# Hybrid SSD/attention/MoE block: half of adaLN's second part moves from TensorE products to VectorE products

## The chip, the cores and the metric

One core of a Trainium2 chip runs the whole block: one sequence of 256 tokens, width 1024, all arrays float32 in memory, batch 1. The metric is the device time of one execution in microseconds. Three runs of the kernel before gave 686.21, 688.96 and 686.09 us (median 686.21 us).

## The reference

```python
def _hybrid_layer(h, c, ...):
    ada = silu(c) @ w_ada + b_ada                 # c: 1 x 1024, w_ada: 1024 x 6144
    shift1, scale1, gate1, shift2, scale2, gate2 = split(ada, 6)
    hn = rmsnorm(h, norm1_g) * (1 + scale1) + shift1
    z, xbc, dt, q, kc, vc, ks, vs, kw, vw, gn, gs, ga = split(hn @ w_in)   # w_in: 1024 x 9040
    y_ssm = mamba2_mixer(z, xbc, dt, ...) @ w_ssm_out     # 4 groups of 8 heads, chunks of 128
    y_nsa = nsa_mixer(q, kc, ...) @ w_nsa_out             # 16 heads; compressed, selected, window
    merged = sigmoid(gs) * y_ssm + sigmoid(ga) * y_nsa
    h = h + gate1 * (merged @ w_o)
    hn2 = rmsnorm(h, norm2_g) * (1 + scale2) + shift2
    return h + gate2 * hier_moe(hn2, ...)                 # 32 experts of hidden 256, top 2
```

The first part of adaLN (shift1, scale1) is needed before anything else can run. The second part, the 4096 columns of gate1, shift2, scale2 and gate2, is needed only from the residual (gate1) and the router and experts (the other three) on. The change concerns these 4096 columns: one row vector of 1024 times a 1024 x 4096 matrix, 16 MB of weights.

## The kernel before, in words

**Stages.** The kernel runs in this order: adaLN's first part and the first columns of `hn @ w_in`; q, k, v (`pj` banks, L612); the last of `xbc` with rope beside it (L1105 to L1107); then one long list of items (L1168 to L1327) in which TensorE computes the projections z, gs, ga, then `no` (w_nsa_out), `so` (w_ssm_out) and `wo` (w_o); then the router; then 16 pairs of experts.

**Items.** A projection of 256 columns ("unit", 1 MB of weights) is two items, one for each 128 columns (`fm_items`, L544). An item first has its weights split (`split`, L216) into a high part on ScalarE (`wh`, L227) and the rest on VectorE (`wl`, L228, 128 x 1024); then 24 matmuls of 128 x 256 run on TensorE (L563 to L565). `project` (L524) traces the split of an item two items ahead of its matmuls. There are three buffers for `wl`.

**Side work.** Beside the items runs one chain of generators (L1105): rope, compression, dt, the compressed attention, the attention over 16 heads (`side_attn`, 36 steps and a last one), and the scan (`side_ssd`, four groups of nine steps, after each second group four more with `ssd_norm`: 44 steps). `weave` (L570) traces, behind every item, 1.5 side steps while the attention lasts (RATE_ATTN) and 1.35 after it (RATE_SSD). It counts items, whatever an item costs: an item with no projection in it, such as a unit of adaLN, also moves the side on by 1.5 or 1.35 steps. So the list of items sets how far the side work stands ahead of or behind the projections in the program.

**Order on the engines.** From this program order the framework fixes one order for each engine: of the instructions that it expects to be ready, the one traced first goes first. Up to the experts no order is written out by hand. `turn_over` (L1217), the item after the first halves of so0 to so2, traces what is left of the side work, closes the buffers of this phase and opens those for the router and experts; its first instruction on GpSimd is at L1232.

**adaLN's second part.** `ada_units` (L185) has 16 units of 256 columns: units 0 to 3 are gate1, 4 to 7 shift2, 8 to 11 scale2, 12 to 15 gate2. The units' weights are streamed two behind each z unit (L193 to L197). `ada_use` (L1142) takes one unit: `ada_rows` (L345) does eight matmuls with the column `sc` (silu(c) in one of 32 columns, the others zero) as stationary operand, on four 32-column strips of the array, into PSUM bank 7; ScalarE copies the four partial rows out (L1148), and a DMA on SP's queue writes them to `adR` in device memory (L1149). The items list has two of these behind each of z0 to z7 (L1185). Behind z7 comes `ada_out` (L1151): it loads `adR`, adds the four partial rows and the bias on 32 partitions, writes the sum to `adD` and transposes it into `a2`. `router_weights` (L1131) comes behind gs3 (L1190).

**Slots.** All weights and most large tiles share 19 slots of 1 MB (L118); a weight's DMA starts when a slot that was released earlier comes free.

Of the kernel before, what the change touches and what calls it, by code (L numbers as in the profile page):

```python
# [12 lines left out]
AF = mybir.ActivationFunctionType  # L13
OP = mybir.AluOpType
# [43 lines left out]
def tile_hybrid_block(ctx: ExitStack, tc: tile.TileContext, x, c, positions, w_ada, b_ada, norm1_g, w_in, conv_w,  # L58
# [4 lines left out]
    PE, V, A, G, SP = nc.tensor, nc.vector, nc.scalar, nc.gpsimd, nc.sync  # L63
# [10 lines left out]
    def ps(b, name):  # L74
        return psp.tile([128, 512], F32, tag=f"b{b}", name=name)

    def work(shape, tag, name, bufs=1, dt=F32):
        return wk.tile(shape, dt, tag=tag, bufs=bufs, name=name)

    def const(shape, name, dt=F32):  # L80
        return csp.tile(shape, dt, name=name)
# [4 lines left out]
    def stt(o, a, s, b, op0, op1):  # L86
        return V.scalar_tensor_tensor(o, a, s, b, op0=op0, op1=op1)  # L87

    def tt(o, a, b, op):
        return V.tensor_tensor(o, a, b, op=op)  # L90

    def ts(o, a, s1, op0, s2=None, op1=None):
        if op1 is None:
            return V.tensor_scalar(o, a, s1, None, op0=op0)  # L94
        return V.tensor_scalar(o, a, s1, s2, op0=op0, op1=op1)
# [7 lines left out]
    def mm(o, l, r, start, stop):  # L103
        return PE.matmul(o, l, r, start=start, stop=stop)  # L104
# [17 lines left out]
    def slot(name):  # L122
        tag = free.pop(0)
        tag_of[name] = tag
        return (big if tag[0] == "s" else box["xtra"]).tile([128, 2048], F32, tag=tag, name=name)

    def load_next():
        name, emit = stream[st["next"]]
        held[name] = slot(name)
        emit(held[name])  # L130
        st["next"] += 1

    def pump():
        while st["next"] < len(stream) and len(free) > st["keep"]:
            load_next()
# [5 lines left out]
    def release(*names):  # L141
        for name in names:
            free.append(tag_of.pop(name))
            held.pop(name, None)
        pump()

    def want(name):
        while name not in held:
            load_next()
        return held[name]  # L150
# [9 lines left out]
    def ld(w, width, c0, n, k0=0, nk=8):  # L160
        def f(t):
            SP.dma_start(t[:, 0:nk * n].rearrange("p (k n) -> p k n", k=nk),
                         dram(w, c0 + k0 * 128 * width, [[width, 128], [width * 128, nk], [1, n]]))
        return f
# [20 lines left out]
    ada_units = [(j, u) for j in range(2, 6) for u in range(4)]  # L185

    def ada_stream(n):
        for j, u in ada_units[n:n + 1]:
            stream.append((f"ad{j}{u}", ld(w_ada, 6144, j * 1024 + u * 256, 256)))

    zga = [(f"z{u}", O_Z + u * 256) for u in range(8)] + [(f"{nm}{u}", o + u * 256) for nm, o in
                                                          (("gs", O_GS), ("ga", O_GA)) for u in range(4)]
    for n, (nm, o) in enumerate(zga):  # L193
        stream.append((nm, ld(w_in, IN_W, o, 256)))
        if n < 8:
            ada_stream(2 * n)
            ada_stream(2 * n + 1)  # L197
    for u in range(4):
        stream.append((f"no{u}", ld(w_nsa_out, 1024, u * 256, 256)))
    for kh in range(2):  # L200
# [34 lines left out]
    def rows(q, dst, r0, src, n):  # L235
        q.dma_start(dst[r0:r0 + n, :], dram(src, 0, [[128, n], [1, 128]]))
# [11 lines left out]
    ones = const([128, 128], "ones")  # L248
# [6 lines left out]
    sc = const([128, 8, 32], "sc")  # L255
# [89 lines left out]
    def ada_rows(o, w):  # L345
        wv = w.rearrange("p (k n) -> p k n", k=8)
        for kk in range(8):
            j = kk % 4
            mm(o[32 * j:32 * j + 32], sc[:, kk, :], wv[:, kk, :], kk < 4, kk >= 4)

    def p0_rows(k, t=None):
        b = ps(6, f"ar{k}")
        if t is not None:
            behind(b, t)
        ada_rows(b[:, 0:256], want(f"ada{k}"))
        release(f"ada{k}")
        rw = work([128, 256], "w1k", f"rw{k}", 4)
        V.tensor_copy(rw, b[:, 0:256])
        return rw
# [84 lines left out]
    for k in range(8):  # L444
        if k == 3:
            T2r, T3r, dsk, posi, dtb, alb, w2k, w2v = small_loads()
        if 0 < k < 7:
            rw = p0_rows(k + 1)
        p0_mm(k, 0, *w0)
        if k == 0:  # L450
# [3 lines left out]
            rw = p0_rows(1, w0[1])  # L454
# [12 lines left out]
    b = ps(6, "cols2")  # L467
# [145 lines left out]
    items = []  # L613
# [486 lines left out]
    items = []  # L1100
    for u in range(6):
        def ev(b, u=u):
            conv_silu(*conv_taps(NP0 + 2 * u, b))
# [10 lines left out]
    def z_evac(u, b):  # L1114
        q = SZ[u // 4][:, (u % 4) * 512:(u % 4 + 1) * 512]
        A.activation(q, b, AF.Tanh, scale=0.5)
        stt(q, q, 1.0, b, OP.add, OP.mult)
# [21 lines left out]
    adR = drm.tile([4, 32, 128], F32, name="adR")  # L1139
    adD = drm.tile([32, 128], F32, name="adD")  # L1140

    def ada_use(n):  # L1142
        j, u = ada_units[n]
        b = ps(7, f"adr{n}")
        ada_rows(b[:, 0:256], want(f"ad{j}{u}"))
        release(f"ad{j}{u}")
        rw = work([128, 256], "w1k", f"rwa{n}", 4)
        A.activation(rw, b[:, 0:256], AF.Copy)  # L1148
        SP.dma_start(adR[:, 2 * n:2 * n + 2].rearrange("a r c -> a (r c)"), rw[0:128:32, :])  # L1149

    def ada_out():  # L1151
        aw = work([32, 6, 128], "wA", "aw", 4)
        V.memset(aw[:, 5], 1.0)
        SP.dma_start(aw[:, 0:4], adR.rearrange("a r c -> r a c"))
        rows(SP, aw[:, 4], 0, b_ada[0, 2048:6144], 32)
        rows(SP, aw[:, 5], 16, norm2_g, 8)
        for n in range(1, 5):
            tt(aw[:, 0], aw[:, 0], aw[:, n], OP.add)
        stt(aw[:, 0], aw[:, 0], one16, aw[:, 5], OP.add, OP.mult)
        A.dma_start(adD, aw[:, 0])  # L1160
        b = ps(7, "adT")
        PE.transpose(b[:, 0:32], aw[:, 0], ident[0:32, 0:32])
        V.tensor_copy(a2, b[:, 0:32])

    ada_items = [((lambda: None), (lambda n=n: ada_use(n)), None) for n in range(16)]

    keep(4)
    items = []  # L1168
    for n, (nm, o) in enumerate(zga):
        u = int(nm[-1])  # L1170
        if nm[0] == "z":
            items += fm_items(nm, lambda b, u=u: z_evac(u, b))
        else:
            def ev(b, u=u, nm=nm[:2]):
                if u == 0:
                    box[nm] = slot(nm + "t")
                    if not box.get("attn"):
                        keep(1 if nm == "gs" else 0)
                    elif nm == "ga":
                        keep(3)  # L1180
                A.activation(box[nm][:, u * 512:(u + 1) * 512], b, AF.Tanh, scale=0.5)
            items += fm_items(nm, ev)
            if nm == "ga3":
                items.append(((lambda: None), (lambda: release("HH", "HL")), None))
        items += ada_items[2 * n:2 * n + 2]  # L1185
        if n == 0:
            items.append(((lambda: None), router_loads, None))
        if n == 7:
            items.append(((lambda: None), ada_out, None))
        if n == 11:  # L1190
            items.append(((lambda: None), router_weights, None))

    for u in range(4):
# [200 lines left out]
    b = ps(7, "pos")  # L1394
# [518 lines left out]
```

## Time and profile before

| | before |
|---|---|
| median of 3 runs | 686.21 us |
| the profiled execution's own time | 685.09 us |
| its span, first to last instruction | 683.4 us |
| TensorE matmul busy | 640.0 us (94%) |
| TensorE weight load busy | 507.2 us (74%) |
| VectorE busy | 467.3 us (68%) |
| ScalarE busy | 327.5 us (48%) |
| mean granted TensorE clock | 0.985 |

All times below are microseconds from the first instruction of the profiled execution. Busy shares are of the span; matmuls are pipelined and their ends are modelled, so a busy TensorE can still have room, and its pace is better read from the starts of its matmuls.

### The profile page before, as it was taken

How to read it: one execution, taken by the hardware profiler on the slowest of the kernel's cores; microseconds unless marked ns; L12 is line 12 of the kernel's file. 1: busy time of each engine (PE TensorE's matmuls, PEld its weight loads, DVE VectorE, ACT ScalarE, POOL GpSimd, SP SyncE). 2: the span in 40 equal slices, each digit the busy share in tenths (PEclk: the TensorE clock that was granted, in tenths of full speed). 3: DMA queues.
4: the chain of work that ended last, by engine and by line, in shares of the span. 5: the costliest groups of instructions: out<-in, count | busy, mean ns of one | idle time of the engine just before them, and what ended most of it. 6: DMA issues, size and time to landing. Idle time of an engine off the chain costs nothing. (4 is left out here: it accounts for less than half of the span.)

```text
span 683.4 us, 14362 instructions
## 1 busy us (share of the span) xinstructions
PE 640.0 (94%) x5714; PEld 507.2 (74%) x5715; DVE 467.3 (68%) x1158; ACT 327.5 (48%) x632; POOL 7.9 (1%) x67
## 2 busy tenths in 40 slices
PE   8999999899899999999999999988988999999882
PEld 7889889897767777999899998774655655656541
DVE  3657999994788878786999766574444534555543
ACT  5435878663378667355745544452322312222333
POOL 2000000000000000000000100000000000000000
PEclk9999999999999999999999999999999999999997
DMA  8997971479667758636477998637999999999971
GB/s 267 335 336 242 370 224 54 144 236 300 208 203 252 257 173 277 195 119 237 132 253 241 345 406 299 234 106 299 419 420 420 419 420 420 418 419 419 416 315 63
DMA packets 102196, 193.28 MB, mean 283 GB/s; under 512 B 7636, under 2 KB 83940, under 8 KB 90596
## 3 DMA queue, kind: packets, MB, share of 16 engines
q1 hardware_dynamic: 101268, 191.05, 76.8%
q8 instruction: 57, 0.93, 0.6%
q10 hardware_dynamic: 848, 1.11, 0.5%
q14 instruction: 23, 0.19, 0.1%
HBM read 190.98 MB, written 1.16 MB: 281 GB/s over the span
## 5 line engine op out<-in xcount | busy, mean ns | idle before, releaser
L104 PE MATMUL moe<-g,XG 128*32 128x256 f32 (+1 forms) x560 | 69.4, 380 | 2.4 <-PEq L1590 1.1
L104 PE MATMUL moe<-u,XG 128*32 128x256 f32 (+1 forms) x560 | 69.5, 381 | 0.0
L104 PEld LDWEIGHTS moe<-g,XG 128*32 128x32 f32 (+1 forms) x560 | 39.5, 112 | 28.4 <-issue 10.0
L1575 ACT ACTIVATE moe<-moe 64x256 f32<-64x256 f32 x32 | 11.4, 356 | 67.1 <-DVE hp L94 65.3
L104 PE MATMUL moe<-d,rw 128*32 128x512 f32 (+1 forms) x280 | 38.6, 631 | 2.0 <-ACT XG L1500 1.2
L104 PE MATMUL pj_z<-HH,wl 128*128 128x256 f32 x128 | 36.5, 285 | 0.5 <-DVE wl L90 0.5
L87 DVE SCALAR_TENSOR_TENSOR hp<-hp,moe 64x256 f32<-64x256 f32 x32 | 13.4, 419 | 34.2 <-ACT hp L1611 33.8
L104 PE MATMUL pj_z<-HH,wh 128*128 128x256 f32 x128 | 36.5, 285 | 0.0
L104 PE MATMUL pj_z<-HL,wh 128*128 128x256 f32 x128 | 36.3, 283 | 0.0
L104 PEld LDWEIGHTS moe<-u,XG 128*32 128x32 f32 (+1 forms) x560 | 35.2, 112 | 0.3
L1500 ACT ACTIVATE XG<-moe,GC 128x256 f32<-128x256 f32 x36 | 18.0, 564 | 34.2 <-PE moe L104 34.2
L104 PE MATMUL moe<-DT,HFh 128*128 128x256 f32 x128 | 31.8, 298 | 2.1 <-DVE DT L90 1.1
L1611 ACT ACTIVATE hp<-moe 64x256 f32<-64x256 f32 x32 | 12.1, 379 | 43.9 <-PEq L1590 26.8
L913 ACT ACTIVATE P<-P,mn 128x128 f32<-128x128 f32 (+1 forms) x64 | 28.4, 446 | 5.2 <-DVE mn L910 4.9
L104 PE MATMUL moe<-DT,HFl 128*128 128x256 f32 x128 | 30.6, 288 | 0.2 <-DVE HFl L87 0.2
L104 PE MATMUL pj_xb<-HH,wh 128*128 128x256 f32 x96 | 27.0, 282 | 3.0 <-ACT BC L493 1.5
L104 PEld LDWEIGHTS moe<-DT,HFh 128*128 128x128 f32 x128 | 24.0, 195 | 5.6 <-issue 5.6
L104 PE MATMUL xa<-HH,wh 128*128 128x256 f32 x96 | 27.8, 293 | 0.0
L104 PE MATMUL pj_xb<-HL,wh 128*128 128x256 f32 x96 | 26.8, 279 | 0.0
L104 PE MATMUL pj_xb<-HH,wl 128*128 128x256 f32 x96 | 26.8, 279 | 0.0
L104 PE MATMUL xa<-HL,wh 128*128 128x256 f32 x96 | 26.6, 280 | 0.0
L104 PE MATMUL xa<-HH,wl 128*128 128x256 f32 x96 | 26.3, 282 | 0.0
(478 smaller groups left out, 2011.0 us busy)
## 6 DMA issues: line engine op xcount, KB each, us to landing
g<-in_w_exp_gate_dram SPq DMA_DIRECT2D x30, 1024.0 KB
u<-in_w_exp_up_dram SPq DMA_DIRECT2D x30, 1024.0 KB
d<-in_w_exp_down_dram SPq DMA_DIRECT2D x30, 1024.0 KB
ad<-in_w_ada_dram SPq DMA_DIRECT2D x16, 1024.0 KB
ada<-in_w_ada_dram SPq DMA_DIRECT2D x16, 512.0 KB
z<-in_w_in_dram SPq DMA_DIRECT2D x8, 1024.0 KB
so<-in_w_ssm_out_dram SPq DMA_DIRECT2D x8, 1024.0 KB
qk<-in_w_in_dram SPq DMA_DIRECT2D x8, 936.0 KB
```

Source lines behind the costliest of these rows:

```text
L87: return V.scalar_tensor_tensor(o, a, s, b, op0=op0, op1=op1)
L104: return PE.matmul(o, l, r, start=start, stop=stop)
L913: A.activation(o, o, AF.Exp, bias=mn[:, n:n + 1], scale=-1.0, accum_out=sm[:, n:n + 1])
L1500: A.activation(o, b_, AF.Identity, scale=GC[:, 1, k:k + 1], bias=GC[:, 0, k:k + 1])
L1575: A.activation(B5[h, s * 256:(s + 1) * 256], B5[h, s * 256:(s + 1) * 256], AF.Copy, accum_out=self.ws[h])
L1611: A.activation(th[g], B4[g, s * 256:(s + 1) * 256], AF.Tanh, scale=0.5)
```

## The change

Units 4 to 11 (shift2 and scale2) are taken off TensorE. For such a unit `ada_part` does eight VectorE instructions of 128 x 256: the first multiplies the weights of 128 rows by the column `sc[:, 0]`, each of the other seven multiplies the next 128 rows and adds to the sum so far. The eight come as two items of four. When two units are done, `ada_pair` does one matmul for each with a 128 x 32 block of ones, into two strips of bank 7, which adds over the partitions; one copy and one DMA follow. These rows are complete, so only row 0 of `adR` is written for them; `ada_out` clears its tile and loads the other three partial rows for units 0 to 3 and 12 to 15 alone.

The places move too. The eight units that stay on TensorE (0 to 3, 12 to 15) come two to a z unit, with z0 to z3. The VectorE units come one to a projection unit, with z4 to z7 and gs0 to gs3, the first of each unit's items ahead of the projection's last one. `ada_out` moves from z7 to behind ga0, `router_weights` from gs3 to behind ga3. The list thus has 16 half-unit items and four pair items in the place of eight unit items.

```diff
@@ -190,11 +190,16 @@
 
     zga = [(f"z{u}", O_Z + u * 256) for u in range(8)] + [(f"{nm}{u}", o + u * 256) for nm, o in
                                                           (("gs", O_GS), ("ga", O_GA)) for u in range(4)]
+
+    ada_at = [[] for _ in zga]
+    for i, n in enumerate((0, 1, 2, 3, 12, 13, 14, 15)):
+        ada_at[i // 2].append((n, True))
+    for i, n in enumerate(range(4, 12)):
+        ada_at[4 + i].append((n, False))
     for n, (nm, o) in enumerate(zga):
         stream.append((nm, ld(w_in, IN_W, o, 256)))
-        if n < 8:
-            ada_stream(2 * n)
-            ada_stream(2 * n + 1)
+        for m, _ in ada_at[n]:
+            ada_stream(m)
     for u in range(4):
         stream.append((f"no{u}", ld(w_nsa_out, 1024, u * 256, 256)))
     for kh in range(2):
@@ -1148,10 +1153,37 @@
         A.activation(rw, b[:, 0:256], AF.Copy)
         SP.dma_start(adR[:, 2 * n:2 * n + 2].rearrange("a r c -> a (r c)"), rw[0:128:32, :])
 
+    ada_sum = {}
+
+    def ada_part(n, half):
+        j, u = ada_units[n]
+        w = want(f"ad{j}{u}").rearrange("p (k n) -> p k n", k=8)
+        if not half:
+            ada_sum[n] = work([128, 256], "w1k", f"as{n}", 4)
+        o = ada_sum[n]
+        for kk in range(4 * half, 4 * half + 4):
+            if kk:
+                stt(o, w[:, kk], sc[:, kk, 0:1], o, OP.mult, OP.add)
+            else:
+                ts(o, w[:, 0], sc[:, 0, 0:1], OP.mult)
+        if half:
+            release(f"ad{j}{u}")
+
+    def ada_pair(n):
+        b = ps(7, f"adr{n}")
+        for i in range(2):
+            mm(b[32 * i:32 * i + 32, 0:256], ones[:, 0:32], ada_sum.pop(n + i), True, True)
+        rw = work([128, 256], "w1k", f"rwa{n}", 4)
+        A.activation(rw[0:64], b[0:64, 0:256], AF.Copy)
+        SP.dma_start(adR[0, 2 * n:2 * n + 4].rearrange("(a r) c -> a (r c)", a=2), rw[0:64:32, :])
+
     def ada_out():
         aw = work([32, 6, 128], "wA", "aw", 4)
+        V.memset(aw[:, 1:6], 0.0)
         V.memset(aw[:, 5], 1.0)
-        SP.dma_start(aw[:, 0:4], adR.rearrange("a r c -> r a c"))
+        SP.dma_start(aw[:, 0], adR[0])
+        for r0 in (0, 24):
+            SP.dma_start(aw[r0:r0 + 8, 1:4], adR[1:4, r0:r0 + 8].rearrange("a r c -> r a c"))
         rows(SP, aw[:, 4], 0, b_ada[0, 2048:6144], 32)
         rows(SP, aw[:, 5], 16, norm2_g, 8)
         for n in range(1, 5):
@@ -1162,7 +1194,16 @@
         PE.transpose(b[:, 0:32], aw[:, 0], ident[0:32, 0:32])
         V.tensor_copy(a2, b[:, 0:32])
 
-    ada_items = [((lambda: None), (lambda n=n: ada_use(n)), None) for n in range(16)]
+    def ada_items(at):
+        r = []
+        for n, on_pe in at:
+            if on_pe:
+                r.append(((lambda: None), (lambda n=n: ada_use(n)), None))
+            else:
+                r += [((lambda: None), (lambda n=n, h=h: ada_part(n, h)), None) for h in range(2)]
+                if n % 2:
+                    r.append(((lambda: None), (lambda n=n: ada_pair(n - 1)), None))
+        return r
 
     keep(4)
     items = []
@@ -1182,12 +1223,14 @@
             items += fm_items(nm, ev)
             if nm == "ga3":
                 items.append(((lambda: None), (lambda: release("HH", "HL")), None))
-        items += ada_items[2 * n:2 * n + 2]
+        extra = ada_items(ada_at[n])
+        items[-1:-1] = extra[:1]
+        items += extra[1:]
         if n == 0:
             items.append(((lambda: None), router_loads, None))
-        if n == 7:
+        if n == 12:
             items.append(((lambda: None), ada_out, None))
-        if n == 11:
+        if n == 15:
             items.append(((lambda: None), router_weights, None))
 
     for u in range(4):
```

## Rows read from the trace of the kernel before

**Rows 1.** Stretches: busy of each engine (instructions), TensorE clock, DMA share, GB/s.
```profile
105.00:150.00 45.00, 41.36 (x343) 39.80 (x342) 43.07 (x80) 34.14 (x57) 0.00 (x0) 1.00 0.51 164
...
193.00:272.00 79.00, 78.76 (x719) 57.81 (x718) 65.00 (x280) 58.26 (x171) 0.00 (x0) 1.00 0.72 235
272.00:389.00 117.00, 116.58 (x1007) 106.94 (x1007) 98.87 (x182) 61.17 (x80) 0.00 (x0) 1.00 0.64 219
193.00:389.00 196.00, 195.34 (x1724) 164.75 (x1723) 163.87 (x461) 119.43 (x249) 0.00 (x0) 1.00 0.67 225
430.00:470.00 40.00, 35.75 (x278) 26.95 (x280) 22.95 (x82) 17.58 (x34) 0.00 (x0) 0.98 0.44 153
470.00:660.00 190.00, 175.93 (x1916) 109.14 (x1912) 97.14 (x246) 49.74 (x129) 0.00 (x0) 0.98 1.01 418
```

**Rows 2.** Single tiles: nanoseconds least, median, most; first and last start.
```profile
L1116 ACT ACTIVATE SZa<-pj_z x4: 581/598/600, 160.9 to 193.3; 128x512 f32<-128x512 f32 x4
...
L104 PE MATMUL adr<-ad,sc x256: 379/379/403, 164.6 to 271.5; 128*32 128x256 f32 x128
...
L104 PE MATMUL pj_gs<-HH,wh x64: 277/280/684, 273.2 to 302.1; 128*128 128x256 f32 x64
...
L104 PE MATMUL rb<-rs,ident x8: 376/376/479, 326.5 to 385.5; 64*128 64x256 f32 x8
```

**Rows 3.** Order of time, GpSimd: the first instruction of `turn_over`.
```profile
389.15 0.21 POOL L1232 MEMSET G<- 128x128 f32 x1 [292.90 <-PE pj_so L104]
```

**Rows 4.** Order of time, TensorE: start, length, instruction; an adaLN unit, a dense half unit.
```profile
164.40 0.28 PE L104 MATMUL pj_z<-HL,wh 128*128 128x256 f32 x1
164.61 1.07 PE L104 MATMUL adr<-ad,sc 128*32 128x256 f32 x16
165.61 0.39 PE L104 MATMUL pj_z<-HH,wl 128*128 128x256 f32 x1
165.83 0.28 PE L104 MATMUL pj_z<-HH,wh 128*128 128x256 f32 x1
...
290.13 0.28 PE L104 MATMUL pj_gs<-HH,wh 128*128 128x256 f32 x1
...
292.93 0.28 PE L104 MATMUL pj_gs<-HH,wh 128*128 128x256 f32 x1
```

**Rows 5.** The same view, TensorE: one product with ones, in the scan.
```profile
355.61 0.28 PE L104 MATMUL pj_no<-OL,wh 128*128 128x256 f32 x1
355.82 0.62 PE L104 MATMUL ysq<-y,ones 128*32 128x256 f32 x2
356.37 0.39 PE L104 MATMUL pj_no<-OH,wl 128*128 128x256 f32 x1
```

**Rows 6.** VectorE groups, 193 to 389: busy, mean ns, idle before, releaser.
```profile
L90 DVE TENSOR_TENSOR wl<-so,wh 128x1024 fp32r<-128x1024 f32 x8 | 9.8, 1219 | 2.0 <-ACT wh L227 2.0
L94 DVE TENSOR_SCALAR P<-P,sm 128x256 f32<-128x256 f32 x32 | 9.7, 346 | 0.0
...
L90 DVE TENSOR_TENSOR wl<-no,wh 128x1024 fp32r<-128x1024 f32 x8 | 9.7, 1218 | 1.2 <-ACT wh L227 1.2
...
L87 DVE SCALAR_TENSOR_TENSOR SZa<-XSa,SZa 128x256 f32<-128x256 f32 x8 | 3.0, 418 | 0.0
...
L87 DVE SCALAR_TENSOR_TENSOR gat<-gat,pj_no 128x512 f32<-128x512 f32 x4 | 2.7, 677 | 0.0
```

**Rows 7.** Order of time, VectorE: independent products, a chain, a wait.
```profile
177.19 0.19 DVE L94 TENSOR_SCALAR po<-po 128x64 f32<-128x64 f32 x1
177.41 0.23 DVE L90 TENSOR_TENSOR po<-po,s 128x64 f32<-128x64 f32 x1
...
243.24 0.17 DVE L94 TENSOR_SCALAR sm<-sm 128x4 f32<-128x4 f32 x1 [1.09 <-ACT P L913]
...
290.57 0.75 DVE L87 SCALAR_TENSOR_TENSOR SZa<-XSa,SZa 128x256 f32<-128x256 f32 x2
```

## The prediction

> **What bounds the kernel now.** I read the busy shares by stretch first [rows 1]; the stretch that matters is taken from where single tiles start and end. z0 to z3 are done at 193.3, where the last tanh of SZa starts; `turn_over`'s first instruction on GpSimd starts at 389.15 [rows 2, 3]. In these 196 us TensorE is busy 195.3, VectorE 163.9, ScalarE 119.4, and the transfers take 67% of the DMA engines [rows 1]. Busy says little of TensorE, so I look at its starts: 24 matmuls of a half unit go out from 290.13 to 292.93, 2.80 us, 0.117 each, no gap between [rows 4]. In the stretch TensorE is the bound; VectorE has 32.1 us of idle time.
>
> An earlier stretch shows the other regime. From 105 to 150 VectorE is busy 43.1 of 45 us (96%) and TensorE issues 343 matmuls (131 ns each, transposes among them) [rows 1]: there VectorE sets the pace.
>
> A gain or loss at `turn_over` reaches the end unchanged: from 430 to 470 the DMA engines are busy 44%, since the slots are full of expert weights, and from 470 to 660 they are full (1.01, 418 GB/s) [rows 1]. That stretch can begin only when the experts begin to free slots, so it moves with them.
>
> **The change part by part.** *TensorE, removed.* A unit stands between the matmuls at 164.40 and 165.83: 1.43 us, in which two matmuls of z would have taken 0.23. It costs 1.20 us (0.09 before it, 1.00 itself, 0.11 after it) [rows 4]. Eight units: 9.6 us.
>
> *TensorE, added.* One product with ones takes 355.61 to 356.37, 0.76 us, of which one matmul's 0.12 would have passed anyhow, and the matmul behind it loses 0.11 as behind a unit: 0.75 [rows 4, 5]. A pair has two products on two strips: at least 0.75, at most 1.30 if they don't overlap (0.55 more, 355.82 to 356.37). In a unit, four strips overlap well, so I take 0.8. Four pairs: 3.2 us (3.0 to 5.2). Net TensorE is freed 6.4 us (4.4 to 6.6).
>
> *VectorE, added.* Eight units of one scalar product and seven multiply-adds, all 128 x 256 from SBUF. The nearest row is SZa<-XSa,SZa: 418 ns for one, but two independent ones take 0.75 together, so 0.33 from start to start [rows 6, 7]. Here each multiply-add needs the one before; in a chain the next starts after the full length and some 0.03 more (177.19 plus 0.19, next at 177.41) [rows 7], so 0.45, unless other work is put between. The first of a unit is nearest to P<-P,sm, 0.35 [rows 6], which I take as 0.27 to 0.38 by the same overlap or pause. Sum: 56 x 0.33 + 8 x 0.27 = 20.6 to 56 x 0.45 + 8 x 0.38 = 28.2 us. I take 24, as some will be interleaved. The larger memset in `ada_out` has 640 columns, less than the 1.22 us of a 1024-column instruction [rows 6]: 0.5.
>
> So in 193 to 389 VectorE's work goes from 163.9 to 188.4 us (184.5 to 193.3), TensorE's from 195.3 to 188.9. If the two fitted together without a gap, the stretch would take 189 us in the place of 196. That is the most that the change can bring, and it would need both engines full for 189 us at once.
>
> *What is moved: the side work.* Behind every item 1.5 or 1.35 side steps are traced, so half units and pairs move the side work on as projections do. I counted items and steps in the program. Up to z7 nothing shifts much: before and after, the attention ends with z7's last items (trace: units' last start 271.5, gs from 273.2 [rows 2]). The scan's 44 steps, however, stand before from `ada_out` to so20's first half, beside 29 half units (gs 8, ga 8, no 8, so 5); the trace agrees, since norm's last product starts at 385.5 [rows 2]. Afterwards the eight half items of gs and the two pairs there pull it forward: it runs from z7's last items to the second half of no0, beside 18 half units (gs 8, ga 8, no 2). Twelve half units (no1 to no3, so00 to so20) are left behind it with no side work.
>
> Twelve half units alone cost TensorE 12 x 2.80 = 33.6 us and VectorE little: six of eight splits of `no` (7.3), six or more of `so` (all eight run before 389: 9.8), three of four results of `no` (2.0) [rows 6], 19.1 us in all. What stands in the program ahead of them is for VectorE 163.9 - 19.1 + 24.5 = 169.3 us, for TensorE 188.9 - 33.6 = 155.3. By program order VectorE is the bound there. At the 96% that it reached from 105 to 150 it needs 176 us, to 369. If no later half unit ran ahead, 33.6 us more would follow: 403, 13.6 later than before. TensorE has 176 - 155 = 21 us free in that time; each later half unit that fits in costs VectorE about 1.6 us (19.1/12) and takes 2.8 off the tail, a net 1.2 with VectorE full, and the whole 2.8 where VectorE would have waited.
>
> How many fit? A split needs a moment in which nothing older is ready on VectorE. There are some: once a head VectorE waits about 1.09 us for the exponentials (243.24) [rows 7]; but the additions of adaLN, older in the program, take these first: 32.1 us of idle time before, 24.5 of it taken. I take five of the twelve, two of them in VectorE's own gaps: 403 - 2 x 2.8 - 3 x 1.2 = 393.8, 4.7 us later than 389.15. More than that I don't take, since a blocked sum holds the splits behind it in VectorE's queue.
>
> *Weighed with a rule.* The Trainium skill ("Perfetto Trace Analysis", Identifying the Most-Contended Engine) says that matmul busy is no measure of TensorE's room and that its weight-load share is, with occupancy for VectorE. By it TensorE (164.8 of 196 loading weights) and VectorE (163.9) would be equally full now [rows 1], and TensorE's 6.4 us would give nothing back. The starts 0.117 apart [rows 4] contradict it in the projections: there is no room between them.
>
> *Costed at nothing.* ScalarE: four copies fewer, 39% idle. SP's queue: 12 writes of rows in the place of 16, and three loads in `ada_out` in the place of one; a pair's write waits for its chain, product and copy, and the weight loads queue behind it. Loads run at 67% of the DMA engines here, and that hides it; without that cover a delayed slot costs its 1 MB at 418 GB/s, 2.5 us, for four pairs 10. `ada_out` and `router_weights` come later, but what they make is used only after `turn_over`. Two of the four buffers that the sums share with the scan's small tiles are held over two units; the scan's use of them is short. TensorE's clock stays at 1.00 where VectorE sets the pace (105 to 150) [rows 1].
>
> **The sum.** The profiled execution took 685.09, 1.1 less than the median of the three runs (686.21). 685.1 + 4.7 = 689.8 on its own scale, 690.9 on the median's. I say 691.
>
> **The rivals.** *A. VectorE sets the pace, some projections run ahead* (forecast): two to six of the twelve half units run ahead, 3.5 to 11 us slower: 690 to 697.
>
> *B. The gaps take the sums* (faster). The additions have no one waiting soon, the 32 us of idle time hold 24 us of them, and the projections run ahead as needed, so that TensorE stays dense; its 6.4 us come off: 679.8. For it: with TensorE dense VectorE's waits are spread over the whole stretch. Against it: 188.4 us of VectorE work in 190 leaves no gap, where 96% was the most seen over 45 us. It decides at about ten of the twelve half units run ahead; with nine the time is that of before.
>
> *C. Both even out*: eight or nine half units run ahead and the loss of order eats the 6.4 us: 683 to 689.5. By the rule of the Trainium skill (page and section above), with TensorE's relief worth nothing and the sums in VectorE's gaps, it would end here too.
>
> *D. Program order is kept strictly*: no half unit runs ahead, 13.6 us later, and with chains at 0.45 (4 us more) 17.6: 697 to 704. For it: from 105 to 150 TensorE lost time and nothing filled it [rows 1]. Against it: the scan has waits of its own.
>
> *E. The sums don't overlap at all with the waits on weights* (a sum blocked on a late DMA holds the splits): up to 10 us on top of A, 701; counted in D.
>
> **Chances.** A 0.50, B 0.19, C 0.23, D with E 0.08. Under 0.5% (3.4 us) is no change that the measurement tells: 682.8 to 689.6. Faster 0.19, same 0.23, slower 0.58. The range leaves out the lower half of B and the upper half of D: 681 to 703; A's own is 690 to 697.
>
> **What would show it.** Right: VectorE at 95% or more from about 200 to 370 and TensorE's starts looser there; scan's last product (rb) well before 385 while `no` has begun only; afterwards half units at 2.80 us with VectorE half idle; `turn_over` at about 394. The units' 1.0 us gone eight times, pairs at 0.8, sums at 0.33 to 0.45. Wrong: `no` and `so` running beside the scan as before, TensorE dense at 0.117, `turn_over` at 383 (B); or VectorE below 90% with waits on ScalarE or DMA in its queue (E).

## The result and the profile after

The changed kernel takes 714.86 us (median of 4 runs, 713.12 to 718.39), the kernel before 686.15 us: a ratio of 1.042, 95% interval 1.0386 to 1.0453. It is 28.7 us slower. The prediction said 691 us, with 703 as the upper end: the direction came true, the size did not. The profiled execution took 714.87 us, its span is 713.1 us (before 683.4).

The stretches of the changed kernel, with the columns of [rows 1]: busy time of TensorE's matmuls, its weight loads, VectorE, ScalarE, GpSimd (instructions), granted TensorE clock, DMA share, GB/s.

```profile
193.00:272.00 79.00, 78.46 (x631) 60.95 (x629) 69.08 (x285) 50.89 (x156) 0.00 (x0) 0.99 0.56 178
272.00:389.00 117.00, 102.08 (x787) 84.67 (x784) 104.33 (x225) 56.97 (x78) 0.00 (x0) 0.91 0.60 195
...
193.00:389.00 196.00, 180.54 (x1414) 145.62 (x1413) 173.40 (x509) 107.86 (x233) 0.00 (x0) 0.94 0.58 188
...
300.00:310.00 10.00, 7.29 (x40) 5.64 (x41) 9.65 (x20) 4.40 (x6) 0.00 (x0) 0.66 0.18 50
...
330.00:340.00 10.00, 5.79 (x20) 4.28 (x20) 10.00 (x24) 4.16 (x5) 0.00 (x0) 0.50 0.35 107
...
389.00:417.00 28.00, 28.00 (x243) 28.00 (x242) 16.97 (x17) 11.70 (x12) 0.20 (x2) 1.00 0.93 343
```

From 193 to 389 TensorE issues 1414 matmuls in the place of 1724 [rows 1]. The units that went account for 112 of that (128 products less 16 with ones); the other 198, at 0.117 each, are 23 us of work that is late. TensorE is idle 15.5 us where it was idle 0.7. VectorE has more to do (173.4 against 163.9 us) and is the fuller of the two in some slices: from 330 to 340 it is busy all the time, while TensorE issues 20 matmuls at half clock. From 389 on the picture turns: TensorE is dense and VectorE 61% busy (16.97 of 28).

A full VectorE alone does not make that slice. In the kernel before VectorE is busy all the time from 330 to 340 too, and TensorE issues 83 matmuls beside it:

```profile
330.00:340.00 10.00, 9.58 (x83) 9.38 (x82) 10.00 (x26) 7.72 (x9) 0.00 (x0) 1.00 0.44 142
```

A smaller part is late before 193 already. From 150 to 193, with the first sum at 217.5, the changed kernel issues 351 matmuls in the place of 390, and later stretches make up for some of it (from 193 to 219 it issues 243, the kernel before 226). The second line is that of e4_ahead, the changed kernel with a longer look-ahead, of which more below:

```profile
150.00:193.00 43.00, 37.55 (x351) 30.19 (x350) 29.85 (x87) 16.17 (x38) 0.00 (x0) 0.94 0.61 198
...
150.00:193.00 43.00, 40.92 (x403) 34.68 (x402) 32.35 (x90) 17.39 (x39) 0.00 (x0) 1.00 0.70 223
```

`turn_over`'s memset on GpSimd, in the view in order of time, answers to [rows 3]:

```profile
416.80 0.20 POOL L1275 MEMSET G<- 128x128 f32 x1 [320.37 <-PE pj_so L104]
```

It starts 27.65 us later than at 389.15. The spans differ by 29.7, so what was lost by then reached the end nearly unchanged.

Single tiles of the changed kernel answer to [rows 2]: least, median, most ns; first and last start.

```profile
L104 PE MATMUL adr<-ad,sc x128: 379/379/446, 156.2 to 214.6; 128*32 128x256 f32 x128
...
L104 PE MATMUL pj_gs<-HH,wh x64: 277/280/415, 266.0 to 324.2; 128*128 128x256 f32 x64
...
L104 PE MATMUL pj_no<-OH,wh x64: 277/280/281, 375.2 to 399.4; 128*128 128x256 f32 x64
...
L104 PE MATMUL rb<-rs,ident x8: 376/376/479, 325.8 to 385.1; 64*128 64x256 f32 x8
```

The scan's last product (rb) starts at 385.1, where it started at 385.5 before, although the scan was traced beside 18 half units in the place of 29. What it lost is in the projections: gs takes from 266.0 to 324.2, 58 us in the place of 29 [rows 2], and `no` only begins at 375.2.

The list of waits between 193 and 390 has entries that the list of the kernel before does not have, among them these (engine, tile, who is waited for: us, times, longest):

```profile
PE pj_gs L104 <- DVE wl L90: 4.1, 3, 2.8
...
PE pj_ga L104 <- DVE wl L90: 3.2, 1, 3.2
PE pj_ga L104 <- ACT gst L1222: 2.3, 2, 1.6
...
PE pj_gs L104 <- ACT gst L1222: 1.6, 1, 1.6
```

TensorE waits for VectorE's half of a split: 7.3 of its 15.5 us of idle time. Another 3.9 us go to ScalarE's reading of finished gs columns (gst). One of the waits for VectorE in order of time, first VectorE, then TensorE:

```profile
320.40 0.47 DVE L87 SCALAR_TENSOR_TENSOR as<-ad,sc,as 128x256 f32<-128x256 f32 x1
320.80 0.34 DVE L94 TENSOR_SCALAR as<-ad,sc 128x256 f32<-128x256 f32 x1
321.06 0.87 DVE L87 SCALAR_TENSOR_TENSOR as<-ad,sc,as 128x256 f32<-128x256 f32 x2
...
326.51 2.83 DVE L87 SCALAR_TENSOR_TENSOR SZa<-SZa,T,rb 128x256 f32<-128x256 f32 x7
329.29 1.22 DVE L90 TENSOR_TENSOR YLa<-SZa,YHa 128x1024 fp32r<-128x1024 f32 x1
...
334.06 1.21 DVE L90 TENSOR_TENSOR wl<-ga,wh 128x1024 fp32r<-128x1024 f32 x1
```

```profile
335.33 0.58 PE L104 MATMUL pj_ga<-HH,wl 128*128 128x256 f32 x1 [3.25 <-DVE wl L90]
335.71 0.41 PE L104 MATMUL pj_ga<-HH,wh 128*128 128x256 f32 x1
335.92 0.41 PE L104 MATMUL pj_ga<-HL,wh 128*128 128x256 f32 x1
```

From 320 to 334 VectorE works through a few sums and a longer stretch of the scan; the split of ga stands behind them. TensorE has waited 3.25 us when it comes, and goes on at 0.21 from start to start, in the place of 0.117 [rows 4]: the clock of this slice is 0.50, the lower of the two levels.

### The profile page after: what moved, and what is told of

It reads as the page before. It is cut to its first block, busy times and chain, and to the rows that moved or that the text cites. A ratio compares the mean times of both kernels' runs of the same rounds, so it can differ in the third digit from the quotient of the medians.

```text
span 713.1 us, 14192 instructions
## 1 busy us (share of the span) xinstructions
PE 650.1 (91%) x5602; PEld 509.8 (71%) x5603; DVE 490.7 (69%) x1223; ACT 326.1 (46%) x628; POOL 7.5 (1%) x67
## 5 line engine op out<-in xcount | busy, mean ns | idle before, releaser
L104 PE MATMUL moe<-u,XG 128*32 128x256 f32 (+1 forms) x560 | 72.3, 386 | 4.0 <-DMA u<-in_w_exp_up_dram 2.1
L104 PE MATMUL moe<-g,XG 128*32 128x256 f32 (+1 forms) x560 | 71.1, 386 | 2.4 <-PEq L1633 1.5
L104 PEld LDWEIGHTS moe<-g,XG 128*32 128x32 f32 (+1 forms) x560 | 38.5, 113 | 26.7 <-issue 10.6
L104 PE MATMUL moe<-d,rw 128*32 128x512 f32 (+1 forms) x280 | 37.1, 608 | 1.9 <-ACT XG L1543 1.2
L90 DVE TENSOR_TENSOR wl<-so,wh 128x1024 fp32r<-128x1024 f32 x16 | 19.6, 1224 | 20.2 <-PE pj_so L104 10.6
L232 ACT ACTIVATE wh<-so 128x1024 fp32r<-128x1024 f32 x16 | 17.0, 1061 | 23.8 <-PE pj_so L104 18.7
```

The lines of the kernel that those rows point to most:

```text
L232: A.activation(hv, src, AF.Copy)
```

## The experiments

Each ratio is to the kernel before, run in turns on the same chip; differences in microseconds are worked out from the ratios, on 686.15 us (the changed kernel, at 1.042, is 28.8 above it). "Sums" are the products and multiply-adds of the eight units on VectorE.

**1. The order, in the changed kernel (e1_no_shift) and alone in the kernel before (e2_shift_only).** The first takes the half units and pairs beside gs out of the count that moves the side work on; the second puts three empty items behind each of gs0 to gs3 of the kernel before, and changes nothing else.

```diff
+            box["w"] = 0.0 if items[i][0] is still else 1.0
...
-            acc += rate()
+            acc += rate() * box.get("w", 1.0)
...
-                r += [((lambda: None), (lambda n=n, h=h: ada_part(n, h)), None) for h in range(2)]
+                r += [(still if n > 7 else (lambda: None), (lambda n=n, h=h: ada_part(n, h)), None) for h in range(2)]
```

```diff
+        if 8 <= n < 12:
+            items += [((lambda: None), (lambda: None), None)] * 3
```

> As the changed kernel, but the half-unit items beside gs and all pair items no longer move the side work on, so that the scan's 44 steps stand beside gs, ga, no and so again, as before the change. Theory O (the order: the items pull the scan ahead, VectorE then sets the pace to no0 and twelve half units follow alone) expects most of the 28.7 us back: 684 to 692 us, turn_over near 389, no first half unit at about 335 to 340. Theory V (the sums cost their time wherever they stand, VectorE has no room for 24 us) expects 704 to 715. Theory L (the added items halve the distance in projections at which splits are traced, so TensorE waits for wl) expects 703 or more, since that is left as it is.

> The kernel before, all sixteen units on TensorE, with twelve empty items put behind the units gs0 to gs3 (three each), which do nothing but move the side work on as far ahead as in the changed kernel. Theory O expects 685 to 691: ahead of the end of the scan there is then 145 us of VectorE work and 162 of TensorE work, so TensorE stays the bound and the order alone costs little. If the order alone were the cause, 700 to 712. Theory L expects 690 to 700, as the empty items shorten the distance of the splits too.

Measured: e1 701.21 us (ratio 1.0187, 1.0129 to 1.0245), e2 690.71 (1.0039, 1.0012 to 1.0066). e1 gives back 16 of the 28.8 us, which lies between theories O and V and below what L allows; 12.8 stay. The order alone, with VectorE as free as before, costs 2.7 us (the empty items shorten the look-ahead beside gs as well, see 2). The tiles of e2 show that the shift is what the prediction took it for:

```profile
L104 PE MATMUL rb<-rs,ident x8: 376/376/479, 314.4 to 362.9; 64*128 64x256 f32 x8
...
L104 PE MATMUL pj_no<-OH,wh x64: 277/278/385, 355.3 to 379.8; 128*128 128x256 f32 x64
```

The scan ends at 362.9, 22.6 us earlier than before [rows 2], and `no` begins at 355.3 in the place of 334.7. So none of the twelve later half units ran ahead here; the loss is small because the scan was that much earlier.

**2. Half of the sums, and the look-ahead.** e3_half_sums does two of the four instructions of each half unit, so that half of the products of shift2 and scale2 are missing. e4_ahead is about `project`: it traces a split two items ahead, and the new items count among these, so that beside z4 to gs3 a split is traced only one projection item ahead. It is made to count projection items alone.

```diff
-        for kk in range(4 * half, 4 * half + 4):
+        for kk in range(4 * half, 4 * half + 2):
```

```diff
+        def ahead(i, j):
+            return sum(r is not None for r in ready[i + 1:j])
...
-            while len(ready) < min(n, i + 1 + AHEAD):
+            while len(ready) < n and (len(ready) <= i or ahead(i, len(ready)) < AHEAD):
```

> As the changed kernel, but each VectorE unit does four of its eight instructions (half of the products are left out of the sums), about 12.5 us less VectorE work in the same places. Theories O and V expect 12 to 15 us less than the changed kernel: 699 to 703. Theory L expects little of it: 710 to 715.

> As the changed kernel, but the two splits that are traced ahead are counted in projection items alone, so that unit and pair items don't shorten the distance. Theory L expects 690 to 702. Theories O and V expect 710 to 716, since VectorE's work and its place are the same.

Measured: e3 704.37 us (1.0234, 1.0177 to 1.0292), e4 704.03 (1.0238, 1.0179 to 1.0297). Half of the sums, some 12 us of VectorE time, give back 12.8 us. The look-ahead gives back 12.5, less than theory L expected and more than O and V did; I had not seen it when I predicted. A part of that falls ahead of the first sum: from 150 to 193 e4 issues 403 matmuls, the changed kernel 351 (both lines above). At 0.117 each that is some 6 us by then, an estimate, and part of it is made up later.

**3. Both corrections, the control, fewer units, no sums.** e5_both is e1 and e4 together. e6_before_ahead is the kernel before with the look-ahead of e4. e7_four is e5 with four units on VectorE (beside z6, z7, gs1 and gs3) and twelve on TensorE. e8_no_sums is the changed kernel with only the first of the eight instructions of each unit, so that shift2 and scale2 are not computed.

```diff
-    for i, n in enumerate((0, 1, 2, 3, 12, 13, 14, 15)):
+    for i, n in enumerate((0, 1, 2, 3, 8, 9, 10, 11, 12, 13, 14, 15)):
         ada_at[i // 2].append((n, True))
-    for i, n in enumerate(range(4, 12)):
-        ada_at[4 + i].append((n, False))
+    for i, n in zip((6, 7, 9, 11), range(4, 8)):
+        ada_at[i].append((n, False))
```

```diff
-        for kk in range(4 * half, 4 * half + 4):
+        for kk in range(4 * half, 4 * half + (not half)):
```

> All eight units on VectorE, with both corrections at once: the added items don't move the side work on, and splits are traced two projections ahead whatever stands between. If the order and the look-ahead are the two causes and add up, 714.9 - 13.7 - 10.9 = 690: 687 to 694. Theory V (VectorE has no room for 25 us beside a dense TensorE) expects that the two overlap and 697 to 702 is left. That the change pays once both are mended (TensorE's 6.4 us come off) would be 679 to 684.

> Control: the kernel before, with the splits counted two projections ahead as in the other kernel (its adaLN items behind z0 to z7 shorten the distance too). If the look-ahead matters only where VectorE is short, 684 to 688; if it matters by itself, 676 to 683.

> Both corrections, and four units on VectorE in the place of eight (shift2, beside z6, z7, gs1 and gs3; the other twelve on TensorE with z0 to z5). TensorE freed 4.8 - 1.6 = 3.2 us, VectorE 12.7 more, about 177 of 196 us. Theory V expects half of what e5 loses: 688 to 694. If there is room for half, 682 to 686.

> The changed kernel with its places, items, pairs and loads, but each VectorE unit does only the first of its eight instructions (the rest of the sum is left out): 25 us of VectorE work gone. If the order and the look-ahead hurt only because VectorE is full, 688 to 694, near the kernel with empty items (690.7) less what TensorE is freed of. If they hurt by themselves, 700 to 708.

Measured: e5 695.52 us (1.0126, 1.0091 to 1.0161), e6 685.38 (0.9977, 0.9958 to 0.9997), e7 689.13 (1.0023, 1.0005 to 1.0041), e8 692.37 (1.0079, 1.0052 to 1.0106). The two corrections together give back 20.2 us, less than the 28.5 of one and the other; the look-ahead does little for the kernel before. Without sums, in the order of the changed kernel, 23.4 us come back: of some 25 us on VectorE over 90% reach the end. e6, e7 and e8 came where one of their theories had them, e5 between the first two of its three. Two stretches of e5:

```profile
273.00:313.00 40.00, 37.68 (x311) 33.42 (x311) 38.29 (x95) 19.84 (x28) 0.00 (x0) 1.00 0.73 238
313.00:353.00 40.00, 35.51 (x278) 30.25 (x276) 35.49 (x70) 22.57 (x31) 0.00 (x0) 0.96 0.67 213
```

From 273 to 313 VectorE is busy 96%, as much as before from 105 to 150 [rows 1], and TensorE issues 311 matmuls.

**4. The relief of TensorE by itself (e12_both_no_sums).** e5 with the sums left out as in e8, so that shift2 and scale2 are not computed.

> Both corrections, and each VectorE unit does only the first of its eight instructions (the rest of the sum is left out): what the relief of TensorE is worth if the sums cost nothing. Forecast by the terms: 687 - 6.4 = 681, 678 to 684. If the relief gives nothing back, 686 to 689.

Measured: 680.93 us, ratio 0.9906 (0.9877 to 0.9934). The same two stretches and `turn_over`'s memset:

```profile
273.00:313.00 40.00, 40.00 (x364) 35.95 (x363) 33.41 (x68) 20.15 (x29) 0.00 (x0) 1.00 0.79 245
313.00:353.00 40.00, 39.82 (x339) 36.60 (x339) 35.39 (x68) 22.81 (x29) 0.00 (x0) 1.00 0.63 208
```

```profile
384.85 0.21 POOL L1283 MEMSET G<- 128x128 f32 x1 [287.31 <-DMA u<-in_w_exp_up_dram]
```

In the same 80 us TensorE issues 703 matmuls in the place of 589. Without the sums the change, with both corrections, is worth 6.4 us (0.94%; the interval is 4.5 to 8.4 us). The longer look-ahead is part of that, and alone it was worth 1.6 us in the kernel before (e6). With the sums in the same order, 15 us come on top. e8, which differs from e12 by the two corrections alone, is 11.9 us slower: so order and look-ahead also hurt by themselves, more than the 2.7 us of e2 let expect.

**5. The sums on other engines.** e9_pool is the changed kernel with the sums on GpSimd, as a product in place and an addition; e10_pool_both the same on e5; e11_act_pool has the products on ScalarE and the additions on GpSimd, on e5.

```diff
-                stt(o, w[:, kk], sc[:, kk, 0:1], o, OP.mult, OP.add)
+                G.tensor_scalar(w[:, kk], w[:, kk], sc[:, kk, 0:1], None, op0=OP.mult)
+                G.tensor_tensor(o, o, w[:, kk], op=OP.add)
```

```diff
-                stt(o, w[:, kk], sc[:, kk, 0:1], o, OP.mult, OP.add)
+                A.activation(w[:, kk], w[:, kk], AF.Copy, scale=sc[:, kk, 0:1])
+                G.tensor_tensor(o, o, w[:, kk], op=OP.add)
```

> The changed kernel, its order and look-ahead, with the sums of the eight units on GpSimd (product into the weights' own place, then an addition): 64 products and 56 additions leave VectorE. If VectorE's work is what costs, the time comes near the kernel that leaves the sums out (692.4): 690 to 697, as long as GpSimd keeps up. If a sum's latency or its place in the program were the cause, it stays at 705 or more, since GpSimd's instructions take longer. If GpSimd slows VectorE's own instructions (a port that both use), 698 to 710, and VectorE's 128x1024 subtraction longer than 1.22 us.

> As the kernel with both corrections (695.5), the sums on GpSimd. If VectorE's work is the rest of the loss, 679 to 686: TensorE's 6.4 us come off as far as the order lets them. If not, 692 to 697.

> As the one before, but the 64 products on ScalarE (about 0.39 us each, 25 us; it was busy 119 of 196 us before) and only the additions on GpSimd. If VectorE was the only full engine, 679 to 688. If ScalarE's splits come late through it, 690 to 698.

Measured: e9 737.82 us (1.0736, 1.0689 to 1.0783), e10 719.25 (1.0466, 1.0419 to 1.0512), e11 696.61 (1.0138, 1.0093 to 1.0183). GpSimd's groups and one of VectorE's in e9 between 193 and 440, then what SP's queue waited for in that time:

```profile
L1166 POOL TENSOR_SCALAR ad<-ad,sc 128x256 f32<-128x256 f32 x56 | 62.2, 1124 | 133.6 <-DVE mn L915 111.1 <-DMA ad<-in_w_ada_dram 22.5
L1167 POOL TENSOR_TENSOR as<-as,ad 128x256 f32<-128x256 f32 x56 | 43.9, 807 | 0.8
...
L94 DVE TENSOR_SCALAR P<-P,sm 128x256 f32<-128x256 f32 x32 | 15.1, 512 | 0.0
```

```profile
SPq L162 <- POOL as L1167: 70.2, 6, 20.0
...
SPq L1014 <- POOL as L1167: 19.1, 1, 19.1
```

A product and an addition take 1.93 us on GpSimd, against 0.48 for the multiply-add on VectorE: 114 us in all. A slot of adaLN's weights comes free only after its last addition, and SP's queue, which issues the loads in order, waited 70 us for these, the scan's own loads (L1014) behind them. GpSimd did not keep up, so e9 and e10 do not decide between the theories. In e11, where GpSimd does the additions alone, VectorE's own work grows:

```profile
L90 DVE TENSOR_TENSOR wl<-gs,wh 128x1024 fp32r<-128x1024 f32 x8 | 11.3, 1409 | 3.6 <-ACT wh L232 3.6
...
L87 DVE SCALAR_TENSOR_TENSOR SZa<-XSa,SZa 128x256 f32<-128x256 f32 x8 | 4.7, 606 | 0.0
```

Before, such a split took 1219 ns (as for so and no) and the other 418 [rows 6]. So moving the sums away freed VectorE of less than it seems. But that does not explain why e11 is no faster than e5. From 273 to 313 VectorE is busy 75% in e11, and yet TensorE issues fewer matmuls there than in e5, 275 in the place of 311. The scan's loads (L1022) again waited in SP's queue for GpSimd's additions, and VectorE waited for what they bring (acB):

```profile
273.00:313.00 40.00, 33.28 (x275) 29.50 (x275) 29.86 (x50) 24.45 (x45) 28.48 (x28) 0.96 0.65 203
...
SPq L1022 <- POOL as L1175: 19.9, 2, 10.5
...
L90 DVE TENSOR_TENSOR we<-acB,acum_s 128x8 f32<-128x8 f32 x4 | 0.6, 160 | 5.8 <-DMA acB<-acD 5.8
```

So e11 does not tell either what a VectorE without the sums is worth.

**6. The sums spread out.** In e5 all sums stand between 219 and 316. e13_spread puts half a unit beside each projection from z4 to no3, and the end of adaLN and the router's weights behind no3 (the units' weights are loaded later to match); e14_spread_no_sums is the same order without the sums but for the first product (shift2 and scale2 are not computed). e15_spread_even and e16_even_no_sums are the same pair with the pace of the side work put right: the items beside z4 to z7 move it twice, and empty items stand in the two places that became free.

```diff
+    def spread(i):
+        n, h = 4 + i // 2, i % 2
+        items.insert(len(items) - 1, (still, (lambda: ada_part(n, h)), None))
+        if h and n % 2:
+            items.append((still, (lambda: ada_pair(n - 1)), None))
```

> The kernel with both corrections, its sums spread: half a unit of sums (four products, 1.6 us) beside each of the sixteen projections z4 to z7, gs, ga and no, in the place of a whole unit beside each of the eight from z4 to gs3. The end of adaLN's second part and the router's weights move behind no3. With both corrections all sums stood between 219 and 316, where VectorE was busy 90.4 of 97 us, and the sums cost 14.6 us (695.5 against 680.9). Place (VectorE is too full only where the sums stand): spread over some 160 us the same 25 us find more idle time, and cost 5 to 9 us: 686 to 690. Amount (both engines are near full over the whole stretch, so every microsecond on VectorE costs the same wherever it stands): 693 to 697.

> The same order of items, with the sums left out but for the first product of each unit, so that shift2 and scale2 of adaLN's second part are not computed; VectorE has 25 us less. It gives the time of this order itself. Both theories: 679 to 684, as without the sums before (680.9). If it is well above that, the place of the sums has moved something else (slots held longer, the late end of adaLN), and only its difference to the kernel with spread sums counts: 5 to 9 us by place, 12 to 16 by amount.

> The spread sums once more, with the pace of the side work put right. In the first try none of the spread items moved the side work, though ten items beside z4 to z7 do in the kernel with both corrections; the scan's last product came at 402.9 without sums, in the place of 381.0, and this order alone cost 19 us. Now the five items beside z4 to z7 move it twice each, and empty items stand where the end of adaLN and the router's weights stood. Place (VectorE is too full only where the sums stood): 686 to 690. Amount (every microsecond on VectorE costs the same over the whole stretch): 693 to 697.

> The same order with the sums left out but for the first product of each unit, so that shift2 and scale2 of adaLN's second part are not computed. Both theories: 679 to 684, near the 680.9 of the order with all sums early. Between the two kernels place expects 5 to 9 us, amount 12 to 16.

Measured: e13 707.17 us (1.0308, 1.0287 to 1.0329), e14 700.25 (1.0197, 1.0171 to 1.0223), e15 723.68 (1.0507, 1.0461 to 1.0553), e16 702.76 (1.0207, 1.0164 to 1.0249). None of the four came where either theory had it. Without sums the two orders are 20 to 21 us slower than e12, and for different reasons. In e14 the scan is late (its last rb starts at 402.9, after 381.0 in e12). In e16 it is on time (379.3), but the end of adaLN now stands late in TensorE's queue:

```profile
353.00:389.00 36.00, 25.35 (x187) 20.92 (x185) 28.79 (x55) 15.37 (x19) 0.00 (x0) 0.86 0.93 308
```

```profile
PE adT L1207 <- DVE aw L87: 7.6, 1, 7.6
...
L104 PE MATMUL rb<-rs,ident x8: 376/376/576, 323.0 to 379.3; 64*128 64x256 f32 x8
```

TensorE idles 10.6 of 36 us here, and its longest wait is the 7.6 us for VectorE's end of adaLN (aw) ahead of the transpose adT at 387.7. That is a part of the 21 us; the rest is not explained. The sums cost 7.6 us in the first of these orders, which is in the range that place forecast for this difference (5 to 9), and 20.6 in the second, more than amount's 12 to 16. The two pairs contradict each other, and both orders lose some 20 us by something else, so they settle neither theory.

## Why the prediction was wrong

**TensorE's terms.** That of the units was right: their products are gone after 214.6. That of the pairs, 0.8 us each, was too small. In the changed kernel the two products of a pair do not run on their strips together, as the prediction took it, but apart (first four lines, one product); in e12 they run together (last two):

```profile
276.21 0.28 PE L104 MATMUL pj_gs<-HH,wl 128*128 128x256 f32 x1
276.42 0.62 PE L104 MATMUL adr<-as,ones 128*32 128x256 f32 x2
276.97 0.39 PE L104 MATMUL pj_gs<-HH,wh 128*128 128x256 f32 x1
277.19 0.28 PE L104 MATMUL pj_gs<-HL,wh 128*128 128x256 f32 x1
...
282.20 0.63 PE L104 MATMUL adr<-as,ones 128*32 128x256 f32 x4
282.76 0.39 PE L104 MATMUL pj_gs<-HH,wh 128*128 128x256 f32 x1
```

From 276.21 to 277.19 is 0.98 us, in which two matmuls would have taken 0.23: 0.75 for a product, so 6.0 us for eight in the place of 3.2, and 3.6 us of relief in the place of 6.4. A pair so costs 1.5 us, more than the 1.30 that the prediction set as the most. That e12 measured just the 6.4 of the forecast is in part luck: its interval is 4.5 to 8.4, its pairs run together and its look-ahead is longer.

The rule of the Trainium skill ("Perfetto Trace Analysis", Identifying the Most-Contended Engine) names the weight-load share beside the share of the peak FLOP rate. The prediction used the first alone and read from it that this relief would be worth nothing. That does not hold here: weight loads at 84% [rows 1] did not mean room, starts 0.117 apart [rows 4] meant none.

**VectorE's sums** were right: 24 us forecast. One takes 475 ns, more than the 418 of the row that I took as nearest [rows 6]. A nearer row stood in the trace of the kernel before, a multiply-add with a column (dcol):

```profile
L87 DVE SCALAR_TENSOR_TENSOR XSa<-XSa,dcol,y 128x256 f32<-128x256 f32 x8 | 3.5, 476 | 0.8 <-PE y L104 0.8
```

But two in a chain take 0.87 us together (321.06), so 0.40 from start to start, no more than the independent ones on SZa (seven in 2.83 us at 326.51, 0.39): 56 x 0.40 + 8 x 0.27 = 24.6. The longer step of a chain that the prediction allowed for (0.45) did not show. Its range for VectorE, 184.5 to 193.3, is 185.0 to 192.6 by its own terms; nothing rests on that.

**The side work's shift** was right in its direction. **At `turn_over` a loss is passed on unchanged** was right: 27.65 there, 29.7 at the end of the span.

**The step that failed is "How many fit?", with the 96% that it rests on.** The prediction let VectorE's part of the program's order end at 369 and five of twelve half units run ahead of it. The amount of VectorE's work was right: 169.3 us were forecast ahead of the end of the scan, and up to the scan's last product at 385.1 VectorE was busy 169.5. But that took 192 us, 88% and not 96%, and so ended 16 us after 369. And of the twelve half units (no1 to so20) about one ran ahead, not five. Up to that product TensorE issued 70 matmuls of `no`, or 2.9 half units, of which two are no0; in e8, without the sums, it is 70 as well (second line: the changed kernel, third: e8, the matmuls, weight loads and VectorE instructions of `no` alone):

```profile
193.00:385.10 192.10, 176.64 (x1383) 142.00 (x1381) 169.50 (x501) 105.34 (x230) 0.00 (x0) 0.94 0.57 185
...
340.00:385.07 45.07, 8.67 (x70) 8.38 (x70) 0.69 (x1) 0.99 0.76 248
...
340.00:361.51 21.51, 8.67 (x70) 8.38 (x70) 0.69 (x1) 1.00 0.82 265
```

The 16.1 us and the 9.2 that five half units were to bring, less 2.6 for the one, are 22.7 of the 23.0 that separate 393.8 from 416.8. That e8 has the same count says more: how many half units ran ahead did not follow VectorE's room, which the prediction weighed, but the order in which the items had been traced. In e5, with that order corrected and all the sums, the whole of `no` (last started at 373.8) and five half units of `so` stand ahead of the scan's last product (394.7), as in the kernel before. VectorE was full in some slices (10.00 from 330 to 340) and had gaps elsewhere.

**TensorE's clock was costed at nothing,** as it stayed at 1.00 from 105 to 150. Here it was 0.94 over the stretch: some of TensorE's waits were followed by matmuls at the lower level (0.66 from 300 to 310, 0.50 from 330 to 340). No run separates the price. An estimate from the rows: the 60 matmuls of these two slices at 0.21 in the place of 0.117 are 5.6 us at most.

**What the prediction did not see** is the look-ahead: it counted how the new items move the side work, but not that the same items halve the distance at which splits are traced. A split traced one projection item ahead has the sums of a half unit in front of it. That is not all of it: from 150 to 193, ahead of every sum, the changed kernels with the short look-ahead issue 349 to 365 matmuls (after, e1, e3, e8, e9) and those with the long one 397 to 403 (e4, e5, e7, e10, e11, e12). There the changed list differs by the place of its items alone: beside z0 to z3, too, the first unit now stands ahead of the projection's last item.

**What the sizes are.** Four kernels cross the order and the sums: after, e8, e5 and e12, at ratios of 1.0420, 1.0079, 1.0126 and 0.9906. On 686.15 us, TensorE's relief in the better order is -6.4 us (e12, longer look-ahead included); the order and look-ahead of the change without sums +11.9 (e8 less e12); the sums in the better order +15.1 (e5 less e12); and 8.3 come only when both are there. Each of these has an interval of 2 to 3 us to either side, the last of about 4. Some 2.8 of the 15.1 may be the pairs, whose products run together in e12 and apart in e5 (one at 234.65, the next at 247.38), an estimate from 6.0 and 3.2 above. Together they are 28.9 by the way they are formed, against 28.7 measured.

**The rivals.** D, strict program order, 697 to 704, was the nearest and had 8% with E. It had the mechanism (no half unit runs ahead) and VectorE still at 96%. B decided at ten of twelve half units ahead; there was one.

**What stays open.** Why the sums still cost 15 us of their 25 when order and look-ahead are put right is not settled. That VectorE is 96% busy where they stand (e5, 273 to 313) fits; the kernels that spread them moved too much else to show it, and those that moved them to GpSimd held up the loads. Nor is it settled why order and look-ahead without sums cost 11.9 us in the changed kernel (e8 less e12) and the order alone 2.7 in the kernel before (e2). No version that computes everything and has units on VectorE beats the kernel before: e7 is 0.2% above it. The kernel before with the longer look-ahead (e6) is 0.2% below.

## What to carry to other kernels

An engine's idle time did not tell what work moved there would cost: it was 30% (e13 less e14) to over 90% (the changed kernel less e8) of 25 us, with the order around it, though 32 us were idle. A list of items that paces other things (side work, the distance of look-ahead) changes them with each item added, so count every loop that reads the list before adding to it. Before moving work, time the kernel with the work left out: e12 shows what the best case is worth, and its 6 us pay only if three quarters of the 25 vanish in idle time.

## What was not expected of the hardware

A multiply-add on VectorE whose factor is a column in SBUF took 475 ns for 128 x 256, one with a constant 418 ns [rows 6]. The kernel before had it already (476 ns, the row of XSa above).

Beside GpSimd some of VectorE's instructions are longer and others not. With the sums on GpSimd the 128 x 256 product P<-P,sm took 512 ns on the mean in the place of 346 [rows 6] (up to 883 among its two sizes), while the custom instruction on s (P<-s,maskn) of the same size took 412 ns, and 417 before; GpSimd's own products took 915 to 2764 ns. In e9:

```profile
L94 DVE TENSOR_SCALAR P<-P,sm x64: 272/367/883, 191.7 to 271.9; 128x128 f32<-128x128 f32 x32, 128x256 f32<-128x256 f32 x32
...
L915 DVE CUSTOM_DVE_ANT_0 P<-s,maskn 128x256 f32<-128x256 f32 x28 | 11.2, 412 | 0.0
```

The Trainium skill ("SBUF — State Buffer", SBUF: two separate sides) has VectorE and GpSimd share a pair of ports, which one instruction holds to its end while the other waits; only some kinds of VectorE instructions use it. Times that are unchanged for one kind and longer by up to 0.5 us for another agree with it.
